# First stage of layer 0: the modulation of k tile 15 taken from TensorE to VectorE, in pieces of 256 columns

## The chip, the cores and the metric

The kernel runs on one core of one Trainium2 chip. The metric is the device time of one execution in microseconds (us). TensorE multiplies matrices, VectorE and ScalarE work element by element, GpSimd does a few small operations, and SyncE issues the transfers (DMA) between the device's memory and the core's on-chip memory (SBUF); matmul results land in PSUM, in banks of 512 columns.

## What is computed

A trunk of two mixer layers over 256 latent and 256 context tokens of width 2048, in float32. The part that matters here is the start of a layer, for both token streams:

```python
shift, scale, gate = split(silu(c) @ w_mod[l] + b_mod[l], 3)      # silu(c_ctx) for the context stream
h = rmsnorm(x, g_pre[l]) * (1 + scale) + shift
proj = h @ w_in[l]                                                # 2048 x 5120 a layer
y = concatenate(gMLP(proj), window_attention(proj), fourier_mix(proj))
x = x + gate * rmsnorm(y @ w_out[l], g_post[l])
```

`w_mod` is 2048 x 6144 a layer, and `c` has just one row a stream, so that product reads many bytes for little arithmetic.

## The kernel before, in words

Tokens lie along the columns: `h` is kept as 16 k tiles of 128 rows (channels) by 512 columns (256 latent, then 256 context tokens). Every float32 operand of the large products is split into a high and a low part (`hh`/`hl` for `h`, `whi`/`wlo` for weights), and `mm3` multiplies three of the four combinations. ScalarE makes the high part (L401, L505), VectorE the low part (L403, L510).

**The first stage** of layer 0 is the loop over k in `layer(0)`: the pass for one k is called step k here. A step multiplies h tile k with its rows of the weights: 12 matmuls into the four banks `av` and 9 into the three banks `au`. The h tiles are not there beforehand; each is made one step earlier, and for this its scale and shift have to be known. `mod_start` does that for one k tile: it loads 2 MB of `w_mod` (array `wsl`: for each of 16 tiles four blocks of 128 partitions x 4 rows x 256 columns, 128 of the columns scale and 128 shift), multiplies it on TensorE (L169: 16 matmuls a tile, four of them side by side in quarters of 32 columns), turns the result on VectorE (L173), adds the four quarters up with four tiny matmuls against `selq` (L178), and finishes scale (`gs`, L187, L189) and shift (`sh`, L190) on VectorE. `make_h` then makes `w2k` = x * gs * r (L501), `hh` (L505) and `hl` (L510).

From step 5 on, step k runs in this order: the first 6 `av` matmuls; the split of a piece of `w_in` into `whi` and `wlo`; the 16 modulation matmuls of tile k+2 (L169); the four of L178 for tile k+1 and `make_h` of tile k+1; the turn (L173) of tile k+2; the other 6 `av` matmuls; the 9 `au` matmuls.

**What sets the order.** TensorE's order is written out by hand for the whole kernel. VectorE's, ScalarE's and SyncE's are too until step 14, where `first_stage.close()` hands them to the compiler's scheduler; the operations that it may place begin a little before that point. Each engine takes its instructions in order. SyncE issues every load of this stage in order, and each issue waits until its buffer is free and until the eighth load before it has landed. Even tiles load into `mraw`, `mraw`, `macc`, `vv` (512 KB each), odd ones into `mg`, `mgl` and four pieces of 256 KB (in `hh`/`hl`, later `yo`); so the loads of tile k+2 wait for the matmuls of tile k. Pieces of `w_in` (512 KB) go through `raw`, which has 3 buffers, and become `whi`/`wlo`, which have 4 each. `LOADS` and `SPLITS` list how many pieces are loaded and split in each step.

Later modulation (layer 0's gate, layer 1's shift and scale) is done by VectorE already, in `mod_dve`: a running sum over the 16 rows with the element of silu(c) as scalar (L205, L207), then a turn and a reduction (L213, L214).

Of the kernel before, what the change touches and what calls it, by code (L numbers as in the profile page):

```python
# [7 lines left out]
F32 = mybir.dt.float32  # L8
# [3 lines left out]
ALU = mybir.AluOpType  # L12

P = 128
D = 2048
KT = D // P
# [50 lines left out]
def trunk_kernel(ctx: ExitStack, tc: tile.TileContext, xT, xhalf, cT, wss, wsl, wmod, win, wout0, wout1, const, vec, rows,  # L67
                 wmat, bs, sink, out):
    nc = tc.nc
    V, A, G, PE, DMA = nc.vector, nc.scalar, nc.gpsimd, nc.tensor, nc.sync  # L70
# [6 lines left out]
    def sb(shape, dt, tag, bufs=1):  # L77
        cnt[0] += 1
        return pool.tile(shape, dt, tag=tag, bufs=bufs, name=f"{tag}_{cnt[0]}")

    def w2k(shape, dt=F32):
        return sb(shape, dt, "w2k", W2K)
# [5 lines left out]
    def ms_ps(name="ms"):  # L88
        cnt[0] += 1
        return psum.tile([P, 512], F32, tag="ms", bufs=2, name=f"ps_{name}_{cnt[0]}")  # L90
# [12 lines left out]
    cs = sb([P, KT, 2], F32, "cs")  # L103
# [16 lines left out]
    def cc(name):  # L120
        o, w = COFF[name]
        return cst[:, o - P:o - P + w]

    def vc(l, name):
        o, w = VOFF[name]
        return vecs[:, l, o:o + w]
# [5 lines left out]
    gs = [sb([P, KT, 2], F32, f"gs{l}") for l in range(2)]  # L132
    sh = [sb([P, KT, 2], F32, f"sh{l}") for l in range(2)]
# [56 lines left out]
        V.tensor_tensor(out=sh[0][:, sl], in0=v[:, nk:2 * nk], in1=wide(bm[:, sl]), op=ALU.add)  # L190

    banks = {}

    def mod_dve(l, cb, red):

        acc = sb([P, 2, 512], F32, "macc")
        for kg in range(4):
            for kk in range(4):
                if kk % 2 == 0:
                    w = sb([P, 2, 512], F32, "mraw", 2)  # L200
                    DMA.dma_start(w, wmod[(cb - 8) if l == 0 else 4 + cb, kg][:, kk:kk + 2])
                for s in range(2):
                    c = cs[:, kg * 4 + kk, s:s + 1]
                    if kg == 0 and kk == 0:
                        V.tensor_scalar(out=acc[:, s], in0=w[:, kk % 2], scalar1=c, scalar2=None, op0=ALU.mult)  # L205
                    else:
                        V.scalar_tensor_tensor(out=acc[:, s], in0=w[:, kk % 2], scalar=c, in1=acc[:, s],  # L207
                                               op0=ALU.mult, op1=ALU.add)
                if kk % 2 and (kg < 3 or kk < 3):
                    yield  # L210
        t = sb([P, 2, 512], F32, "mraw", 2)
        for s in range(2):
            V.transpose(t[:, s], acc[:, s])  # L213
            V.tensor_reduce(out=red[:, s], in_=t[:, s].rearrange("p (b j) -> p b j", j=32),  # L214
                            axis=mybir.AxisListType.X, op=ALU.add)
        yield
# [264 lines left out]
    def new_h(k):  # L481
        hh[k] = sb([P, T], F32R, f"hh{k}")
        hl[k] = sb([P, T], F32R, f"hl{k}")

    def h_of(l, k, sl):

        if l == 0:
            return hh[k][:, sl], hl[k][:, sl]
        s, a = sl.start // S, sl.start % S
        t, b = (hh, hl)[s][k], a + sl.stop - sl.start  # L490
        return t[:, a:b], t[:, S + a:S + b]

    def make_h(l, k, rb, streams, between=()):

        if streams[0] == 0:
            new_h(k)
        t = w2k([P, T])
        for s in streams:
            sl = slice(s * S, (s + 1) * S)
            rsl = slice((s - streams[0]) * S, (s - streams[0] + 1) * S)  # L500
            V.scalar_tensor_tensor(out=t[:, sl], in0=yo[k][:, sl], scalar=gs[l][:, k, s:s + 1],  # L501
                                   in1=rb[:, rsl], op0=ALU.mult, op1=ALU.mult)
        for s in streams:
            sl = slice(s * S, (s + 1) * S)
            first = A.activation(h_of(l, k, sl)[0], t[:, sl], AF.Identity, bias=sh[l][:, k, s:s + 1])  # L505
        next(iter(between), None)
        for s in streams:
            sl = slice(s * S, (s + 1) * S)
            hi, lo = h_of(l, k, sl)
            last = V.scalar_tensor_tensor(out=lo, in0=t[:, sl], scalar=sh[l][:, k, s:s + 1],  # L510
                                          in1=hi.bitcast(F32), op0=ALU.add, op1=ALU.subtract)
        return first, last
# [58 lines left out]
    def layer(l):  # L571
        last = l == 1
        n = S if last else T
# [3 lines left out]
        if last:  # L577
            a = sb([P, 4, 256], F32, "macc")
            c = [sb([P, 2, S], F32, f"kt{j}") for j in range(2)]
# [35 lines left out]
        if l == 0:  # L615
            made = {}

            def mod_in(k, n=5):
                if k < KT:
                    g = made.setdefault(k, mod_start(k, 1))  # L620
                    for _ in range(n):
                        next(g, None)

            for k in range(KT):
                def take_in(n):
                    mod_in(k + 1, n)

                def splits():
                    for _ in range(SPLITS[k]):
                        W.emit()  # L630

                def h_next():

                    if k + 1 < KT:
                        mod_in(k + 1)
                        make_h(0, k + 1, rb0, [0, 1])

                if k % 2 == 0:
                    take(k)
                if k <= EARLY:  # L640
                    take_in(1)
                if k >= EARLY:
                    mod_in(k + 2, 1)
                for _ in range(LOADS[k]):
                    W.load()
                if k == 0:
                    start_av(0, range(nt))
                    take_in(3)
                    e = W.emitting(512)
                    next(e)  # L650
                    next(e)
                    take_in(2)
                    take(0, (1,))
                    start_au(0, (0,))
                    h_next()
                    list(e)
                    start_au(0, (1,))
                    warm(au[2], 3)
                elif k < MIDDLE:
                    start_av(k, range(nt // 2))  # L660
                    take_in(2)
                    start_av(k, range(nt // 2, nt))
                    take_in(1)
                    splits()
                    take_in(2)
                    start_au(k, (0,))
                    h_next()
                    start_au(k, (1,))
                    if k == 1:
                        warm(au[2], 4)  # L670
                    else:
                        ws_[2] = W.next()
                        for i in range(k + 1):
                            start_au(i, (2,))
                else:
                    start_av(k, range(nt // 2))
                    if k <= EARLY:
                        take_in(3)
                        splits()
                        take_in(2)  # L680
                        start_av(k, range(nt // 2, nt))
                        h_next()
                    else:
                        if k == KT - 2:
                            first_stage.close()
                        if k + 2 < KT:
                            banks["mod", k + 2] = banks["modc", k + 1] = ms_ps("mod")
                        splits()
                        mod_in(k + 2, 4)
                        if k + 1 < KT:  # L690
                            mod_in(k + 1)
                            make_h(0, k + 1, rb0, [0, 1])
                        mod_in(k + 2, 1)
                        start_av(k, range(nt // 2, nt))
                    if k >= KT - 2:
                        for _ in range(2):
                            with low(LAG), tc.issue_after(W.last.ins):
                                next(mods)
                    take(k, (1, 2))
                    start_au(k)  # L700
                    if k == EARLY:
                        mod_in(k + 2, 5)
# [26 lines left out]
        ws = sb([P, 4, P], F32, "ws")  # L729
# [3 lines left out]
        bsb = sb([P, 4, P], F32, "bsb")  # L733
# [193 lines left out]
        for h in range(len(au), 4):  # L927
            ps = tunit1([0])[0] if last else tunit(n, ps=ms_ps("t"))
# [7 lines left out]
        for h in range(4):  # L936
            ps = tunit1([0])[0] if last else tunit(n)
            gate(h, ps)
        state["phase"] = f"cg{l}"
        for g in range(4):  # L940
            ps = tunit1([0])[0] if last else tunit(n)
# [3 lines left out]
        r = sb([P, 4, S], F32, "mgl")  # L945
# [9 lines left out]
        for k in range(KT):  # L955
            if k % 4 == 0:
                w = W.next()
            c = slice((k % 4) * 256, (k % 4 + 1) * 256)
# [9 lines left out]
        for h in range(8):  # L968
            ps = tunit1([0])[0] if last else tunit(n)
# [3 lines left out]
        for h in range(8):  # L973
            ps = tunit1([0])[0] if last else tunit(n)
# [221 lines left out]
    with tc.manual_schedule(engines={EN.PE}):  # L1196
# [12 lines left out]
        for k in range(KT):  # L1209
            q = w2k([P, T])  # L1210
# [3 lines left out]
            c = slice(32 * (k % 4), 32 * (k % 4) + 32)  # L1214
# [10 lines left out]
        ps = ms_ps("rs")  # L1225
# [99 lines left out]
```

## Time and profile before

| | |
|---|---|
| median of 3 runs | 1141.86 us (1141.32 to 1142.33) |
| profiled execution, its own time | 1142.52 us |
| its span, first to last instruction | 1140.8 us |
| granted TensorE clock | 0.998 of full speed |
| TensorE matmul busy | 1126.3 us, 99% of the span |
| VectorE busy | 880.3 us, 77% |
| ScalarE busy | 515.9 us, 45% |
| DMA, mean over the span | 205 GB/s |
| first stage | from about 21 us to 139 us of the span |

The profile names engines PE (TensorE matmul), PEld (its weight load), DVE (VectorE), ACT (ScalarE), POOL (GpSimd) and SP (SyncE; SPq is its queue of DMA issues). A row of the timeline gives the start in the span, the duration, the engine, the line of the kernel, the operation, the tile written and the tiles read, the count, and in brackets the idle time before it and what ended that. A row of the DMA issues gives the count, the size of one and the median time from issue to landing. A row of the windows gives for a stretch of time each engine's busy time (with the number of instructions), the granted clock, the mean busy share of the 16 DMA engines and the bytes moved a second.

### The profile page before, as it was taken

What the parts mean: (1) busy time and instruction counts of PE and PEld (TensorE: products, weight loads), DVE (VectorE), ACT (ScalarE), POOL (GpSimd) and SP (SyncE); (2) the same over time, 40 slices, a digit from 0 to 9 for tenths busy, and PEclk for the clock granted to TensorE, in tenths of its full rate; (3) what the DMA queues carried; (4) which work ended last, traced back from release to release, by engine and by line L of the source; (5) the groups of instructions that cost most, each with busy time, mean ns of one, the idle gap of its engine ahead of it and who ended that gap; (6) DMA issues with size and microseconds to landing.
All of it is one profiled execution on the core that took longest, in us unless ns stands there. A gap on an engine that the chain in (4) does not pass through costs nothing.

```text
span 1140.8 us, 16858 instructions
## 1 busy us (share of the span) xinstructions
PE 1126.3 (99%) x6339; PEld 931.5 (82%) x6339; DVE 880.3 (77%) x1480; ACT 515.9 (45%) x933; POOL 31.6 (3%) x39
## 2 busy tenths in 40 slices
PE   8999999999999999999999999999999999999997
PEld 3567788888898888888888888888888988888885
DVE  1545499999987797889999893395789789868884
ACT  5222422322335666632532323366465369856550
POOL 0000000000000000000000000200500000000001
PEclk9999999999999999999999999999999999999999
DMA  9999666556655343355466654255865786556972
GB/s 351 395 387 404 240 202 198 182 186 218 195 182 169 112 138 130 108 197 189 147 219 217 206 185 149 74 188 185 198 223 180 239 275 194 167 160 199 300 255 74
DMA packets 72658, 234.28 MB, mean 205 GB/s; under 512 B 8448, under 2 KB 11392, under 8 KB 72576
## 3 DMA queue, kind: packets, MB, share of 16 engines
q1 hardware_dynamic: 70272, 231.11, 60.2%
q0 software_dynamic: 2304, 2.10, 1.3%
q8 instruction: 49, 0.80, 0.3%
q14 instruction: 33, 0.27, 0.1%
HBM read 231.08 MB, written 2.10 MB: 204 GB/s over the span
## 4 chain that ended last, share of the span: by engine, by line
PE 92%; DMA 4%; DVE 3%; ACT 1%; issue 1%; POOL 0%; SPq 0%; DVEq 0%; ACTq 0%; POOLq 0%
PE ps_t L423 14%; PE ps_t L425 14%; PE ps_t L424 14%; PE ps_t L539 8%; PE ps_t L540 4%; PE ps_y L423 3%; PE ps_y L425 3%; PE ps_y L424 3%; PE ps_mod L169 2%; PE ps_av L423 2%; PE ps_av L424 2%; PE ps_av L425 2%; PE ps_tp L906 2%; PE ps_cx L423 1%; PE ps_cx L425 1%; PE ps_cx L424 1%
## 5 line engine op out<-in xcount | busy, mean ns | idle before, releaser
L401 ACT CAST whi<-raw 128x1024 fp32r<-128x1024 f32 (+1 forms) x216 | 224.1, 1041 | 327.6 <-PE ps_t L424 186.4
L403 DVE TENSOR_TENSOR wlo<-raw,whi 128x1024 fp32r<-128x1024 f32 (+1 forms) x216 | 260.6, 1211 | 69.4 <-ACT whi L401 67.7
L423 PE MATMUL ps_t<-hh,whi 128*128 128x512 f32 (+1 forms) x704 | 268.2, 381 | 0.0
L425 PE MATMUL ps_t<-hh,wlo 128*128 128x512 f32 (+1 forms) x704 | 267.6, 380 | 0.0
L424 PE MATMUL ps_t<-hl,whi 128*128 128x512 f32 (+1 forms) x704 | 267.4, 380 | 0.0
L207 DVE SCALAR_TENSOR_TENSOR macc<-mraw,cs,macc 128x512 f32<-128x512 f32 x360 | 249.2, 747 | 16.3 <-DMA mraw<-in_wmod_dram 15.9
L539 PE MATMUL ps_t<-hh,whi 128*128 128x512 f32 x448 | 163.4, 402 | 0.0
L425 PEld LDWEIGHTS ps_t<-hh,wlo 128*128 128x128 f32 x704 | 132.4, 188 | 25.2
L423 PEld LDWEIGHTS ps_t<-hh,whi 128*128 128x128 f32 x704 | 132.4, 188 | 24.9 <-issue 1.2
L424 PEld LDWEIGHTS ps_t<-hl,whi 128*128 128x128 f32 x704 | 132.4, 188 | 23.8
L540 PE MATMUL ps_t<-hh,wlo 128*128 128x256 f32 x448 | 125.6, 280 | 0.3 <-DVE wlo L403 0.3
L539 PEld LDWEIGHTS ps_t<-hh,whi 128*128 128x128 f32 x448 | 84.2, 188 | 18.9 <-issue 0.5
L540 PEld LDWEIGHTS ps_t<-hh,wlo 128*128 128x128 f32 x448 | 84.6, 189 | 1.5 <-DVE wlo L403 1.0
L505 ACT ACTIVATE hh<-w2k,sh 128x256 fp32r<-128x256 f32 x48 | 21.8, 502 | 78.0 <-DVE w2k L501 78.0
L423 PE MATMUL ps_y<-whi,hh 128*128 128x512 f32 x104 | 41.3, 397 | 0.0
L425 PE MATMUL ps_y<-whi,hh 128*128 128x512 f32 x104 | 40.6, 390 | 0.0
L424 PE MATMUL ps_y<-wlo,hh 128*128 128x512 f32 x104 | 40.5, 389 | 0.0
L423 PE MATMUL ps_av<-whi,hh 128*128 128x512 f32 x96 | 39.7, 413 | 0.6 <-ACT hh L505 0.6
L423 PE MATMUL ps_cx<-whi,hh 128*128 128x512 f32 x96 | 38.9, 405 | 0.0
L424 PE MATMUL ps_av<-wlo,hh 128*128 128x512 f32 x96 | 38.0, 396 | 0.4 <-DVE wlo L403 0.4
L424 PE MATMUL ps_cx<-wlo,hh 128*128 128x512 f32 x96 | 37.4, 389 | 0.0
L440 ACT CAST w2k<-ps_tp 128x512 fp32r<-128x512 f32 x40 | 23.4, 585 | 23.2 <-PE ps_scc L424 12.7
(398 smaller groups left out, 1861.1 us busy)
## 6 DMA issues: line engine op xcount, KB each, us to landing
raw<-in_win_dram SPq DMA_DIRECT2D x160, 512.0 KB, 4.2
mraw<-in_wmod_dram SPq DMA_DIRECT2D x128, 512.0 KB, 4.4
raw<-in_wout_dram SPq DMA_DIRECT2D x60, 512.0 KB, 4.4
mraw<-in_wsl_dram SPq DMA_DIRECT2D x16, 512.0 KB, 7.4
yo<-in_xT_dram SPq DMA_DIRECT2D x16, 256.0 KB, 5.4
macc<-in_wsl_dram SPq DMA_DIRECT2D x8, 512.0 KB, 7.8
vv<-in_wsl_dram SPq DMA_DIRECT2D x8, 512.0 KB, 8.1
mg<-in_wsl_dram SPq DMA_DIRECT2D x8, 512.0 KB, 8.1
```

Source lines behind the costliest of these rows:

```text
L169: PE.matmul(ps[32 * kk:32 * kk + 32, 0:n], cpad[:, kg * 4 + kk], ws[kk], start=kg == 0, stop=kg == 3, tile_position=(0, 32 * kk))
L207: V.scalar_tensor_tensor(out=acc[:, s], in0=w[:, kk % 2], scalar=c, in1=acc[:, s], op0=ALU.mult, op1=ALU.add)
L401: A.copy(ph, rc)
L403: self.last = V.tensor_tensor(out=pl, in0=rc, in1=ph.bitcast(F32), op=ALU.subtract)
L423: PE.matmul(ps, st[0], mv[0], start=start, stop=False)
L424: PE.matmul(ps, st[0], mv[1], start=False, stop=False)
L425: PE.matmul(ps, st[1], mv[0], start=False, stop=stop)
L440: A.copy(hi, src)
L505: first = A.activation(h_of(l, k, sl)[0], t[:, sl], AF.Identity, bias=sh[l][:, k, s:s + 1])
L539: PE.matmul(ps, w[0], h, start=k == 0, stop=False)
L540: PE.matmul(ps[:, 0:S], w[1], h[:, 0:S], start=False, stop=k == KT - 1)
L906: PE.transpose(tp[:, (2 * j + b) * P:(2 * j + b + 1) * P], src, ident)
```

## The change

Tile 15 no longer goes through `mod_start`. Its 2 MB come as eight loads of 256 KB (`wide_load`, two rows of 256 columns for each partition), one in each of steps 3 to 10, behind the load of the `w_in` piece and ahead of the next tile's modulation loads. VectorE adds each of them in the step after (`wide_step`, steps 4 to 11): four operations on 128 x 256 a step, 32 in all. Behind `make_h` of step 12 it turns and reduces the two sums (`wide_turn`), and in step 14 four tiny matmuls and three small operations finish scale and shift (`wide_end`).

```diff
+    WIDE = {k: 1 for k in range(4, 12)}
+    def wide_load(n):
...
+            w = sb([P, 2, 256], F32, ("nstrh", "nstrl", "ws", "bsb")[i % 4])
+            DMA.dma_start(w, wsl[KT - 1, i // 2][:, 2 * (i % 2):2 * (i % 2) + 2])
...
+    def wide_step(n):
...
+            for k in (2 * i, 2 * i + 1):
+                for s in range(2):
+                    acc, c = wide["acc"][:, s], cs[:, k, s:s + 1]
+                    if k == 0:
+                        V.tensor_scalar(out=acc, in0=w[:, 0], scalar1=c, scalar2=None, op0=ALU.mult)
+                    else:
+                        V.scalar_tensor_tensor(out=acc, in0=w[:, k % 2], scalar=c, in1=acc, op0=ALU.mult, op1=ALU.add)
+    def wide_turn():
...
+        for s in range(2):
+            V.transpose(t[:, s], wide["acc"][:, s])
+            V.tensor_reduce(out=wide["red"][:, 0, s, 0:8], in_=t[:, s].rearrange("p (b j) -> p b j", j=32),
+                            axis=mybir.AxisListType.X, op=ALU.add)
+    def wide_end():
...
+        for q in range(4):
+            PE.matmul(ps[32 * q:32 * q + 32, 0:4], cc("selq"), r[:, :, :, q], start=True, stop=True,
+                      tile_position=(0, 32 * q))
...
             def mod_in(k, n=5):
-                if k < KT:
+                if k < KT - 1:
...
                 for _ in range(LOADS[k]):
                     W.load()
+                wide_load(WIDE.get(k + 1, 0))
+                more = WIDE.get(k, 0)
...
-                        if k + 2 < KT:
+                        if k + 2 < KT - 1:
                             banks["mod", k + 2] = banks["modc", k + 1] = ms_ps("mod")
+                        wide_step((more + 1) // 2)
                         splits()
+                        wide_step(more // 2)
                         mod_in(k + 2, 4)
                         if k + 1 < KT:
                             mod_in(k + 1)
+                            if k == KT - 2:
+                                wide_end()
                             make_h(0, k + 1, rb0, [0, 1])
+                        if k == max(WIDE) + 1:
+                            wide_turn()
```

The helpers stand 52 lines further down than before, the loop some 54 to 61. The order of the instructions moves at three places that the prediction speaks of.

TensorE in step 13, before: between the two halves of the `av` matmuls stand the 16 modulation matmuls of tile 15 (rows of L169) and the four tiny ones for tile 14 (L178).

```order
L425 MATMUL ps_av_280<-whi_1146,hl_257_1244 128x512
L169 MATMUL ps_mod_1289<-mg_1269,kt_24_87 32x256 x4
L169 MATMUL ps_mod_1289<-mgl_1271,kt_24_87 32x256 x4
L169 MATMUL ps_mod_1289<-yo_262_1273,kt_24_87 32x256 x2
L169 MATMUL ps_mod_1289<-yo_263_1275,kt_24_87 32x256 x2
L169 MATMUL ps_mod_1289<-yo_264_1277,kt_24_87 32x256 x2
L169 MATMUL ps_mod_1289<-yo_265_1279,kt_24_87 32x256 x2
L178 MATMUL ps_mod_1289<-w2k_1252,cst_79 32x4 x4
L423 MATMUL ps_av_281<-whi_1146,hh_256_1243 128x512
```

The same place now:

```order
L476 MATMUL ps_av_280<-wlo_1196,hh_265_1292 128x512
L477 MATMUL ps_av_280<-whi_1195,hl_266_1293 128x512
L178 MATMUL ps_modc_1336<-w2k_1307,cst_79 32x4 x4
L475 MATMUL ps_av_281<-whi_1195,hh_265_1292 128x512
L476 MATMUL ps_av_281<-wlo_1196,hh_265_1292 128x512
```

The 16 matmuls are gone; TensorE's order is otherwise what it was.

SyncE's queue in steps 5 and 6, before: a piece of `w_in`, the four loads of tile 8, another piece, the first loads of tile 9.

```order
L381 DMA raw_707<-in_win_dram 128x1024
L162 DMA mraw_769<-in_wsl_dram 128x1024
L162 DMA mraw_771<-in_wsl_dram 128x1024
L162 DMA macc_773<-in_wsl_dram 128x1024
L162 DMA vv_775<-in_wsl_dram 128x1024
L381 DMA raw_777<-in_win_dram 128x1024
L162 DMA mg_839<-in_wsl_dram 128x1024
```

The same place now, with two of the eight loads for tile 15 (L202, into `ws` and `bsb`):

```order
L433 DMA raw_716<-in_win_dram 128x1024
L202 DMA ws_718<-in_wsl_dram 128x512
L162 DMA mraw_784<-in_wsl_dram 128x1024
L162 DMA mraw_786<-in_wsl_dram 128x1024
L162 DMA macc_788<-in_wsl_dram 128x1024
L162 DMA vv_790<-in_wsl_dram 128x1024
L433 DMA raw_792<-in_win_dram 128x1024
L202 DMA bsb_794<-in_wsl_dram 128x512
L162 DMA mg_860<-in_wsl_dram 128x1024
```

Each tile's loads now stand behind one more load of 256 KB; tile 15's own six loads behind tile 14's are gone.

ScalarE and VectorE at the end of the stage. ScalarE before: the high part of tile 13, tile 14 with one weight piece between them (`whi`), two weight pieces, tile 15.

```order
L505 ACTIVATE hh_256_1243<-w2k_1245,sh_28_92 128x256 x2
L401 CAST whi_1290<-raw_1211 128x1024
L505 ACTIVATE hh_270_1317<-w2k_1319,sh_28_92 128x256 x2
L401 CAST whi_1352<-raw_1281 128x1024
L401 CAST whi_1408<-raw_1343 128x1024
L505 ACTIVATE hh_278_1364<-w2k_1366,sh_28_92 128x256 x2
```

ScalarE now (`m0r` is the attention mask):

```order
L557 ACTIVATE hh_265_1292<-w2k_1294,sh_28_92 128x256 x2
L453 CAST whi_1332<-raw_1260 128x1024
L453 CAST whi_1377<-raw_1324 128x1024
L453 CAST whi_1433<-raw_1368 128x1024
L557 ACTIVATE hh_275_1344<-w2k_1346,sh_28_92 128x256 x2
L557 ACTIVATE hh_282_1389<-w2k_1391,sh_28_92 128x256 x2
L786 CAST m0r_1475<-w2k_1473 128x128
```

VectorE there before, from the turn of tile 14 to the low part `hl` of tile 14:

```order
L173 STREAM_TRANSPOSE w2k_1252<-ps_mod_1219 128x256
L403 TENSOR_TENSOR wlo_1291<-raw_1211,whi_1290 128x1024
L187 SCALAR_TENSOR_TENSOR gs_26_90<-ps_mod_1289,vecs_78 128x2
L189 TENSOR_TENSOR gs_26_90<-gs_26_90,vecs_78 128x2
L190 TENSOR_TENSOR sh_28_92<-ps_mod_1289,vecs_78 128x2
L501 SCALAR_TENSOR_TENSOR w2k_1319<-yo_15_75,gs_26_90,acc_241 128x256 x2
L510 SCALAR_TENSOR_TENSOR hl_271_1318<-w2k_1319,sh_28_92,hh_270_1317 128x256 x2
```

VectorE now:

```order
L173 STREAM_TRANSPOSE w2k_1307<-ps_mod_1268 128x256
L455 TENSOR_TENSOR wlo_1333<-raw_1260,whi_1332 128x1024
L187 SCALAR_TENSOR_TENSOR gs_26_90<-ps_modc_1336,vecs_78 128x2
L455 TENSOR_TENSOR wlo_1378<-raw_1324,whi_1377 128x1024
L189 TENSOR_TENSOR gs_26_90<-gs_26_90,vecs_78 128x2
L190 TENSOR_TENSOR sh_28_92<-ps_modc_1336,vecs_78 128x2
L553 SCALAR_TENSOR_TENSOR w2k_1346<-yo_15_75,gs_26_90,acc_241 128x256 x2
L455 TENSOR_TENSOR wlo_1434<-raw_1368,whi_1433 128x1024
L562 SCALAR_TENSOR_TENSOR hl_276_1345<-w2k_1346,sh_28_92,hh_275_1344 128x256 x2
```

Two more weight splits now stand in front of tile 14's `hh` on ScalarE and in front of its `hl` on VectorE; they stood behind them before.

More of the change, by code (lines that the diff above doesn't have):

```diff
@@ L192, in trunk_kernel, with both @@
     banks = {}
+    wide = {"n": 0, "w": []}
+    WIDE = {k: 1 for k in range(4, 12)}
+    def wide_load(n):
+        for _ in range(n):
+            i = wide["n"]
+            wide["n"] += 1
+            w = sb([P, 2, 256], F32, ("nstrh", "nstrl", "ws", "bsb")[i % 4])
+            DMA.dma_start(w, wsl[KT - 1, i // 2][:, 2 * (i % 2):2 * (i % 2) + 2])
+            wide["w"].append((i, w))
+    def wide_step(n):
+        if "acc" not in wide:
+            wide["acc"] = sb([P, 2, 256], F32, "ctrh")
+        for _ in range(n):
+            i, w = wide["w"].pop(0)
+            for k in (2 * i, 2 * i + 1):
[6 more added lines that the diff above has]
+    def wide_turn():
+        wide["red"] = sb([P, 4, 2, 16], F32, "red", 2)
+        t = sb([P, 2, 256], F32, "nstrh")
+        for s in range(2):
[3 more added lines that the diff above has]
+    def wide_end():
+        ps = ms_ps("modc")
+        r = wide["red"][:, 0, :, 0:8].rearrange("p s (j q) -> p s j q", q=4)
+        for q in range(4):
+            PE.matmul(ps[32 * q:32 * q + 32, 0:4], cc("selq"), r[:, :, :, q], start=True, stop=True,
+                      tile_position=(0, 32 * q))
+        v = ps[:, 0:4].rearrange("p (s j) -> p j s", s=2)
+        k, bm = KT - 1, vc(0, "bmod")
+        def both(c):
+            return c.to_broadcast([P, 2])
+        V.scalar_tensor_tensor(out=gs[0][:, k], in0=v[:, 0], scalar=1.0, in1=both(bm[:, KT + k:KT + k + 1]),
+                               op0=ALU.add, op1=ALU.add)
+        V.tensor_tensor(out=gs[0][:, k], in0=gs[0][:, k], in1=both(vc(0, "gpre")[:, k:k + 1]), op=ALU.mult)
+        V.tensor_tensor(out=sh[0][:, k], in0=v[:, 1], in1=both(bm[:, k:k + 1]), op=ALU.add)
     def mod_dve(l, cb, red):
@@ L678, in layer @@
                         take_in(3)
+                        wide_step(more)
                         splits()
```

## The prediction

> **What bounds the kernel now.** I read the page's busy table first, then TensorE's waits over the whole span, then the windows and TensorE's timeline of the first stage, then the issues and landings of its loads. Page, then TensorE's waits (total us, times, longest):
>
> ```profile
> span 1140.8 us, 16858 instructions
> PE 1126.3 (99%) x6339; PEld 931.5 (82%) x6339; DVE 880.3 (77%) x1480; ACT 515.9 (45%) x933; POOL 31.6 (3%) x39
> ...
> PE ps_t L539 <- DVE hl L510: 1.0, 1, 1.0
> PE ps_rs L1215 <- ACT w2k L1211: 0.9, 1, 0.9
> PE ps_rs L461 <- DVE acc L1167: 0.7, 1, 0.7
> ```
>
> TensorE has work for 99% of the span and no wait longer than about 1 us after the opening: what the first stage gains or loses on TensorE passes to the end nearly one to one. So everything hangs on TensorE between 50 and 139 us. The windows of that stretch (DMA share and GB/s stand last):
>
> ```profile
> 52.00:54.00 2.00, 2.00 (x33) 1.08 (x26) 0.99 (x2) 0.00 (x0) 0.00 (x0) 1.00 1.06 327
> 54.00:56.00 2.00, 2.00 (x16) 1.39 (x15) 0.66 (x5) 0.00 (x0) 0.00 (x0) 1.00 0.89 341
> ...
> 60.00:62.00 2.00, 2.00 (x25) 1.24 (x18) 0.45 (x1) 0.00 (x0) 0.00 (x0) 1.00 0.73 246
> ...
> 64.00:66.00 2.00, 2.00 (x25) 1.21 (x27) 1.00 (x3) 1.60 (x3) 0.00 (x0) 1.00 0.97 328
> ...
> 70.00:90.00 20.00, 20.00 (x179) 14.78 (x175) 11.09 (x28) 5.65 (x10) 0.00 (x0) 1.00 1.03 407
> 90.00:110.00 20.00, 20.00 (x175) 14.75 (x171) 10.85 (x27) 5.56 (x9) 0.00 (x0) 1.00 1.04 403
> ```
>
> TensorE never stops, but the DMA engines are full as well from 70 us on, at 403 to 407 GB/s. The stage has two bounds a hair apart.
>
> **What goes: 16 matmuls.** TensorE's timeline, start of the second `av` half of steps 12, 13 and 14:
>
> ```profile
> 118.69 0.50 PE L423 MATMUL ps_av<-whi,hh 128*128 128x512 f32 x1
> ...
> 125.61 0.50 PE L423 MATMUL ps_av<-whi,hh 128*128 128x512 f32 x1
> ...
> 130.81 0.50 PE L423 MATMUL ps_av<-whi,hh 128*128 128x512 f32 x1
> ```
>
> From 118.69 to 125.61 (6.92 us) stand 21 main matmuls, 16 modulation matmuls (tile 15) and four tiny ones; from 125.61 to 130.81 (5.20 us) the same without the 16. The change turns the first kind into the second: **−1.72 us**, the whole of what can be won. Step 14 keeps its four tiny matmuls, now fed by `wide_end`.
>
> **What is added to the load queue.** The 2 MB are the same, but they come earlier: eight loads of 256 KB ahead of tiles 5 and 7 to 13, in a stretch where the DMA engines have nothing left. At 405 GB/s one takes 0.26 MB / 0.405 = 0.65 us, and whatever stands behind it lands that much later. The idle shares above give some of it back: against 1.03, they lack 0.28 us (54 to 56), 0.60 (60 to 62) and 0.12 (64 to 66), together 1.0 us; counted by bytes against 405 GB/s, with 52 to 54, they lack 1.9 us. That is room for two or three of the first three loads, and none after it. Whether TensorE feels the rest is read from the last load of a tile, against the matmuls that need it. Tile 10: issue, time to landing, use; then tile 11 and tile 13, whose last matmul group starts 0.22 us before the tiny matmuls (16 matmuls take 1.05 us in four groups):
>
> ```profile
> 80.36 0.33 SPq L162 DMA_DIRECT2D vv<-in_wsl_dram  x1
> vv<-in_wsl_dram SPq DMA_DIRECT2D x1, 512.0 KB, 9.0
> 90.40 0.40 PE L169 MATMUL ps_mod<-vv,kt 128*32 128x256 f32 x4
> ...
> 88.09 0.33 SPq L162 DMA_DIRECT2D yo<-in_wsl_dram  x1
> yo<-in_wsl_dram SPq DMA_DIRECT2D x1, 256.0 KB, 7.8
> 97.75 0.22 PE L178 MATMUL ps_mod<-w2k,cst 128*32 128x4 f32 x8
> ...
> 101.06 0.33 SPq L162 DMA_DIRECT2D yo<-in_wsl_dram  x1
> yo<-in_wsl_dram SPq DMA_DIRECT2D x1, 256.0 KB, 7.8
> 110.74 1.05 PE L169 MATMUL ps_mod<-yo,kt 128*32 128x256 f32 x16
> 111.61 0.22 PE L178 MATMUL ps_mod<-w2k,cst 128*32 128x4 f32 x8
> ```
>
> Tile 10's last load lands at 89.4 and is used at 90.40: 1.0 us to spare. Tile 11's lands at 95.9, used at 97.53: 1.6. Tile 13's lands at 108.9, used at 111.39: 2.5. Ahead of them stand five, six and eight of the new loads: 3.25, 3.9 and 5.2 us, less 1.0 to 1.9. So tile 10 comes 0.35 to 1.25 us late, tile 11 no later than that, and tile 13 0.8 to 1.7 us (the lateness is one delay that grows, not a sum, since a TensorE that waited once has moved back for all later tiles). I take **+1.2 us**, the middle for tile 13. Ends for the range: 0 if the queue finds more room than its idle shares show, 2.7 (5.2 − 2.5) if it finds none.
>
> By the Trainium skill, "DMA: Bandwidth & Descriptors", Specifications, about 358 GB/s is the limit of a core on the memory side; by that figure a load would take 0.73 us and tile 13 would come up to 3.4 us late. The rows at 403 to 407 GB/s disagree, and the page's own single-core measurement of large transfers lies above 400 too.
>
> **What is added to VectorE.** The nearest rows for the new operations, and VectorE around step 11, where two weight splits leave the least room:
>
> ```profile
> L501 DVE SCALAR_TENSOR_TENSOR w2k<-yo,gs,acc 128x256 f32<-128x256 f32 x28 | 12.3, 482 | 0.0
> L214 DVE TENSOR_REDUCE red<-mraw 128x16 f32<-128x512 f32 x24 | 15.7, 670 | 0.1
> ...
> 107.28 0.44 DVE L173 STREAM_TRANSPOSE w2k<-ps_mod 128x256 f32<-128x256 f32 x1
> 107.82 2.36 DVE L403 TENSOR_TENSOR wlo<-raw,whi 128x1024 fp32r<-128x1024 f32 x2
> 111.98 0.16 DVE L187 SCALAR_TENSOR_TENSOR gs<-ps_mod,vecs 128x2 f32<-128x2 f32 x1 [1.80 <-PE ps_mod L178]
> ```
>
> Two operations of 128 x 256 on three operands are 12.3 / 14 = 0.88 us, so the four of a step take 1.76 to 1.93 us. In step 11 VectorE waits 1.80 us for TensorE's tiny matmuls; the four fit there, or are 0.13 us over. In the other steps one split stands instead of two, so 1.2 us more is free. Cost: **0**, hidden by that wait, and where TensorE itself is late by the queue the wait is longer still; without the cover the worst is 0.13 us, and never a gain. The pieces themselves land in time: each stands right behind the weight piece and is first needed a step later. The turn in step 12 is two of 0.44 us and two reductions of at most 0.67 (half the columns), 1.6 to 2.2 us, in a step whose VectorE otherwise only turns tile 14 and splits one piece: 0, at worst 0.2 if the turn of tile 14 comes behind TensorE.
>
> **What is moved at the end of the stage.** ScalarE's third `whi` of those rows may only be written when step 13 has used the buffer's old piece, and tile 14's `hh` and `hl` now stand behind it. Durations and TensorE's clock there:
>
> ```profile
> L401 ACT CAST whi<-raw 128x1024 fp32r<-128x1024 f32 x11 | 11.2, 1037 | 0.0
> L403 DVE TENSOR_TENSOR wlo<-raw,whi 128x1024 fp32r<-128x1024 f32 x11 | 13.2, 1220 | 1.0 <-ACT whi L401 0.5
> L510 DVE SCALAR_TENSOR_TENSOR hl<-w2k,sh,hh 128x256 fp32r<-128x256 f32 x28 | 12.4, 484 | 2.5 <-ACT hh L505 2.4
> ...
> 120.31 0.88 DVE L510 SCALAR_TENSOR_TENSOR hl<-w2k,sh,hh 128x256 fp32r<-128x256 f32 x2 [0.18 <-ACT hh L505]
> ...
> 127.11 0.39 PE L423 MATMUL ps_au<-hh,whi 128*128 128x512 f32 x1
> 129.16 0.39 PE L423 MATMUL ps_av<-whi,hh 128*128 128x512 f32 x1
> ```
>
> Call E the end of step 13's second `av` half (127.11 before, 125.39 without the 16 matmuls). Step 14 starts at E + 2.05 (129.16 − 127.11) and needs `hl` of tile 14 in its third matmul, at E + 2.5. VectorE: tile 13's `hl` is done at 121.19, E − 4.2; the turn and reductions bring it to E − 2.5, the turn of tile 14 to E − 2.1, the first split to E − 0.9, `gs`, the second split and `sh` to E + 0.7, `w2k` to E + 1.6. The third `whi` is ready at E + 1.04, so it does not delay the third split, which ends at E + 2.8; the first half of `hl` follows at E + 3.3. TensorE waits **+0.8 us** there. `hh`, at E + 1.8, is in time. Ends: 0.3, if the operations overlap by 0.1 us each, as back-to-back rows do (0.88 for two of 0.48); 1.4, if reductions and waits on its own results take the upper values. Before, `hl` stood in front of both splits.
>
> Later stages: TensorE's order is unchanged there; VectorE's sums for the gate move by some places around 140 to 190 us, with TensorE waiting for none of them: 0, plus or minus 0.5.
>
> **Sum.** −1.72 + 1.2 + 0 + 0.8 = +0.3 us on the profiled execution, whose 1142.52 us are its span of 1140.8 and 1.7 around it, 0.66 above the median. On the median: 1141.86 + 0.3 = **1142.2 us**.
>
> **The rivals.** Within 0.2% (2.3 us, about what a measurement of this kernel can tell from no change) means 1139.6 to 1144.1.
>
> *The gain arrives whole.* The queue takes up all eight loads and tile 14's `hl` is in time: −1.72 to −1, about 1140.4 us. For it: the landings hold 1.0 to 2.5 us of spare time. Against it: five to eight loads of 0.65 us are more than that. Even then it is 0.15%, no faster than 0.2%.
>
> *The loads cost by count, not by bytes (slower).* If a load of 256 KB holds the queue nearly as long as one of 512 KB (1.3 us at 405 GB/s), eight take 10.4 us; less 1.9 of idle and 2.5 spare, tile 13 comes 6.0 us late, and with 0.8 of tile 14: −1.72 + 6.0 + 0.8 = +5, 1147 us. It decides from 0.9 us a load: 8 x 0.9 − 1.9 − 2.5 = 2.8, and 2.8 + 0.8 − 1.72 is 1.9, with the upper end for tile 14 already 2.5. Against it: tiles of six loads and tiles of four took turns at 403 and 407 GB/s. The Trainium skill's rule ("DMA: Bandwidth & Descriptors", Rules for kernel authors: at least 1 MiB a DMA for the highest bandwidth) speaks for this rival; the windows above, full at that rate with loads of 256 and 512 KB, show no such loss.
>
> *No spare room in the queue.* 2.7 + 0.8 to 1.4 − 1.72 = +1.8 to +2.4: 1143.7 to 1144.3 us, on the edge of 0.2%.
>
> *Later order.* VectorE's other order beyond 140 us moves a wait elsewhere: plus or minus 3 us.
>
> **Chances.** Forecast (−1 to +1.7) 0.60; gain whole 0.16; no room 0.12, half of it over the edge; by count 0.05; later order 0.07, split 0.03 faster, 0.04 slower. Two hundredths of the whole gain may add up with later order to pass the edge. Faster 0.05, slower 0.06 + 0.05 + 0.04 = 0.15, same 0.80. The range runs from the gain kept nearly whole, 1140.3, to the upper end without room, 1144.3.
>
> **What would show it.** In the profile of the changed kernel: L169's matmuls 16 fewer; step 13 5.2 us long; DMA still full at 403 to 407 GB/s from 60 to about 110 us and empty earlier than before; TensorE's weight loads for tile 10 and tile 13 (L169) waiting for a DMA, about 1.2 us in all; the third `av` matmul of step 14 waiting about 0.8 us for `hl`; VectorE's wait ahead of L187 short in steps 5 to 11 but not gone. I am wrong if L169 waits for nothing or for over 2.7 us, if `gs` is late in step 11, or if TensorE's gaps past 140 us change by more than 0.5 us.

## The result and the profile after

The changed kernel takes 1145.74 us (median of 20 runs, 1143.85 to 1150.72), the kernel before 1142.38 us beside it (1141.01 to 1145.03): a ratio of 1.0032, 95% interval 1.0024 to 1.0040. It is slower by 3.4 us, and above the range given.

The profiled execution of the changed kernel took 1143.90 us, the second fastest of its twenty; that of before, 1142.52, lies close to its median. The two profiles differ by 1.4 us, the medians by 3.4: this profile shows less than half of the loss. First what it does show. Its span and busy row:

```profile
span 1142.1 us, 16816 instructions
PE 1126.7 (99%) x6303; PEld 931.0 (82%) x6307; DVE 892.1 (78%) x1515; ACT 516.0 (45%) x933; POOL 31.7 (3%) x39
```

The windows of the first stage (last columns: granted clock, DMA share, GB/s) and the waits from 60 to 132 us (us in total, times, longest), VectorE's wait ahead of `gs` before in a block of its own behind them:

```profile
70.00:90.00 20.00, 20.00 (x163) 14.55 (x157) 15.10 (x40) 5.64 (x10) 0.00 (x0) 1.00 1.03 403
90.00:110.00 20.00, 20.00 (x180) 14.37 (x179) 13.20 (x38) 5.25 (x9) 0.00 (x0) 1.00 1.03 402
...
120.00:130.00 10.00, 10.00 (x70) 7.53 (x58) 8.66 (x21) 4.65 (x7) 0.00 (x0) 1.00 0.52 181
```

```profile
DVE gs L187 <- PE ps_mod L178: 15.4, 8, 4.2
...
PEld ps_mod L169 <- DMA vv<-in_wsl_dram: 0.8, 2, 0.4
...
PEld ps_mod L169 <- DMA yo<-in_wsl_dram: 0.6, 3, 0.3
...
PE ps_av L477 <- DVE hl L562: 0.3, 1, 0.3
```

```profile
DVE gs L187 <- PE ps_mod L178: 26.7, 9, 4.2
```

The queue is full at the same rate, and now TensorE's weight loads of L169 wait for it. VectorE's wait ahead of `gs`, 26.7 us before, still stands at 15.4: the added operations fit. TensorE at the end of the stage (start, duration, idle time before it):

```profile
125.85 0.50 PE L475 MATMUL ps_av<-whi,hh 128*128 128x512 f32 x1
...
129.63 0.40 PE L476 MATMUL ps_av<-wlo,hh 128*128 128x512 f32 x1
130.34 0.50 PE L477 MATMUL ps_av<-whi,hl 128*128 128x512 f32 x1 [0.32 <-DVE hl L562]
```

The third `av` matmul of step 14 waits for tile 14's `hl`. Up to here all is as in the prediction's steps. What was not in them stands 600 us later, in layer 1. ScalarE and TensorE there, before:

```profile
749.61 0.51 ACT L505 ACTIVATE hh<-w2k,sh 128x256 fp32r<-128x256 f32 x1 [1.77 <-DVE w2k L501]
...
750.19 1.05 ACT L401 CAST whi<-raw 128x1024 fp32r<-128x1024 f32 x1
```

and in the changed kernel:

```profile
750.10 0.51 ACT L557 ACTIVATE hh<-w2k,sh 128x256 fp32r<-128x256 f32 x1 [1.76 <-DVE w2k L553]
...
751.46 1.05 ACT L453 CAST whi<-raw 128x1024 fp32r<-128x1024 f32 x1 [0.84 <-DMA raw<-in_win_dram]
...
754.22 0.50 PE L477 MATMUL ps_av<-whi,hh 128*128 128x512 f32 x1 [0.33 <-DVE hh L562]
```

A weight piece arrives late, ScalarE's cast waits 0.84 us for it, and TensorE falls back at 753 us. The change has no instruction anywhere near.

### The profile page after: what moved, and what is told of

Same layout as the page of the kernel before. It is cut to its first block, busy times and chain, and to the rows that moved or that the text cites. A ratio compares the mean times of both kernels' runs of the same rounds, so it can differ in the third digit from the quotient of the medians.

```text
span 1142.1 us, 16816 instructions
## 1 busy us (share of the span) xinstructions
PE 1126.7 (99%) x6303; PEld 931.0 (82%) x6307; DVE 892.1 (78%) x1515; ACT 516.0 (45%) x933; POOL 31.7 (3%) x39
## 4 chain that ended last, share of the span: by engine, by line
PE 89%; DMA 4%; DVE 4%; ACT 2%; issue 1%; SPq 0%; POOL 0%; DVEq 0%; ACTq 0%; POOLq 0%
PE ps_t L475 14%; PE ps_t L477 14%; PE ps_t L476 14%; PE ps_t L591 8%; PE ps_t L592 4%; PE ps_y L475 3%; PE ps_y L477 3%; PE ps_y L476 3%; PE ps_mod L169 2%; PE ps_av L475 2%; DMA raw<-in_win_dram 2%; PE ps_av L477 2%; PE ps_av L476 2%; PE ps_tp L967 1%; PE ps_cx L475 1%; PE ps_cx L477 1%
```

## The experiments

Every run has its median against the kernel before on the same chip, and one profile. To read the profiles, each matmul of a kernel is set beside the same matmul in before's profile; its lateness is its start less the start before, and the table gives by how much TensorE's lateness grows in four stretches (before's times): 51 to 114 us (loads of the first stage), 114 to 150 (the removed matmuls, and tile 14's `hl`), 150 to 760, and 760 to the last common matmul. The last columns are explained with e6. Times in us.

| kernel | ratio to before, 95% | 51–114 | 114–150 | 150–760 | 760–1132 | instruction load at | first `raw` load near 747 took | growth at 753 |
|---|---|---|---|---|---|---|---|---|
| before | 1 | 0 | 0 | 0 | 0 | 742.2 | 3.6 | 0 |
| after | 1.0032 (1.0024–1.0040) | 1.75 | −1.12 | 0.28 | −0.07 | 748.3 | 4.3 | 0.49 |
| e1 | 1.0035 (1.0021–1.0049) | 1.36 | −1.14 | 1.55 | 1.55 | 748.4 | 4.5 | 0.65 |
| e2 | 1.0006 (0.9997–1.0014) | 0.00 | −1.14 | 1.68 | 1.94 | 748.6 | 5.1 | 1.13 |
| e4 | 1.0024 (1.0009–1.0038) | 2.13 | −1.70 | 0.75 | 1.05 | 748.5 | 4.3 | 0.48 |
| e5 | 1.0018 (1.0010–1.0027) | 1.41 | 0.00 | 0.38 | 1.10 | 742.9 | 3.6 | 0 |
| e6 | 1.0007 (0.9997–1.0018) | 2.23 | −1.12 | −0.28 | −1.02 | 742.7 | 3.4 | 0 |
| e7 | 1.0033 (1.0022–1.0045) | 0.23 | 0.00 | 0.99 | 3.28 | 752.3 | 4.8 | 0.89 |
| e7b | 1.0020 (1.0011–1.0028) | 0.00 | 0.00 | −0.13 | 0.13 | 749.9 | 3.5 | 0 |
| e8 | 0.9986 (0.9977–0.9994) | 0.88 | −0.77 | −0.25 | −0.17 | 742.5 | 3.6 | 0 |
| e8 again | 1.0001 (0.9992–1.0009) | 0.86 | −0.77 | −0.28 | −1.07 | 742.0 | 3.7 | 0 |
| e9 | 0.9996 (0.9987–1.0005) | 0.00 | −0.77 | −0.25 | −1.17 | 740.0 | 3.5 | 0 |
| e10 | 0.9991 (0.9982–1.0000) | 1.01 | −1.12 | −0.28 | −0.31 | 741.9 | 3.7 | 0 |
| e11 | 0.9998 (0.9990–1.0007) | 0.00 | −0.78 | −0.27 | 0.52 | 742.2 | 3.6 | 0 |
| e12 | 0.9998 (0.9990–1.0007) | 0.00 | 0.00 | −0.13 | −1.20 | 738.7 | 3.5 | 0 |

The first theory (Q) was that the whole loss is the load queue's, the rival (O) that it is the changed order of VectorE and ScalarE.

**e1**, the changed kernel again.

> The changed kernel itself, unaltered, as a control on the chip of the runs beside it and for a second profile. Theory Q (the eight added loads leave the load queue no spare time, so that what loading varies by from execution to execution becomes waiting of TensorE): about +3.4 us over the kernel before, executions spread over about 7 us where the kernel before has 4; a profile of an execution that takes over 1145 us shows the extra time before 120 us, as waits of L169 or L477 for a DMA. Theory O (the order at the end of the stage or later costs more than the first profile shows): the same time, but the extra time stands after 120 us.

The time repeats (1146.73). Its profile is of an execution of 1145.83 us, and the extra time stands after 150 us, against Q: 3.1 us. One part of it is VectorE's order, as O has it. VectorE and TensorE at 158 to 169 us:

```profile
158.00 0.75 DVE L259 SCALAR_TENSOR_TENSOR macc<-mraw,cs,macc 128x512 f32<-128x512 f32 x1 [1.77 <-DMA mraw<-in_wmod_dram]
...
164.25 4.05 DVE L259 SCALAR_TENSOR_TENSOR macc<-mraw,cs,macc 128x512 f32<-128x512 f32 x6
...
168.22 0.74 DVE L820 SCALAR_TENSOR_TENSOR w2k<-ps_mix,vecs,bsb 128x512 f32<-128x512 f32 x1
...
169.02 1.16 PE L818 MATMUL ps_mix<-ws,w2k 128*128 128x128 f32 x8 [0.74 <-DVE w2k L820]
```

Six sums for the gate now stand in one row ahead of the `w2k` that TensorE needs (before, five did, and that `w2k` waited 0.45 us for TensorE, not the other way round); when a load of `mraw` comes late, TensorE falls back 0.9 us at 168. The order alone does not do it: in the first profile the same kernel has the same six sums, and TensorE does not wait there.

**e2**, one piece instead of eight; **e4**, the hand order closed one step later; **e5**, the kernel before with the eight loads alone.

```
e2  -  w = sb([P, 2, 256], F32, (...)[i % 4]); DMA.dma_start(w, wsl[KT - 1, i // 2][...])
    +  if i == 0:
    +      w = sb([P, 2, 256], F32, "ws"); DMA.dma_start(w, ...); wide["one"] = w
    +  w = wide["one"]
e4  -  if k == KT - 2:
    +  if k == KT - 1:
           first_stage.close()
e5  +  if 3 <= k < 11:                      # behind W.load() of step k
    +      w = sb([P, 2, 256], F32, (...)[(k - 3) % 4]); DMA.dma_start(w, wsl[KT - 1, ...])
```

> The changed kernel with one load of 256 KB instead of eight; all 32 operations of VectorE read that one piece. Left out: seven of the eight loads, so tile 15's modulation is not that of the reference. Theory Q: the 16 matmuls' 1.72 us come back, less 0.5 for tile 14's hl: -1.2 us against the kernel before (1141.2), with its spread of about 4 us. Theory O, or VectorE's added operations as the cause: no change against the changed kernel, about +3.4 us over before.

> The changed kernel with the hand order of the first stage held one step longer (closed at step 14's end of order, not at step 13's), so that tile 14's hh and hl stand ahead of the third pair of weight splits. Theory Q: at most the 0.5 us that the first profile shows as waiting for hl come back, so about +2.9 us over before, spread as wide as the changed kernel's. Theory O: most of the +3.4 us goes, to within 1 us of before.

> The kernel before with the eight loads of 256 KB alone, in steps 3 to 10 where the change has them; nothing reads them, TensorE, VectorE and ScalarE work as before. Theory Q: the 16 matmuls are still there and no hl is late, so the changed kernel's +3.4 plus 1.72 less 0.5: about +4.6 us over before, spread as wide as the changed kernel's. Theory O: no change against before, within 0.5 us.

In the first stage all three do what Q says: without the seven loads nothing waits for a DMA (e2, 0.00) and 1.14 us are gained there; without the late `hl` it is 1.70 (e4); the loads alone cost 1.41 (e5). e4's time, 0.24% over before, is Q's too. But e2's median is 2.1 us above Q's figure (1143.34 for 1141.2), and e5's 0.18% over before, 2.1 us, is less than half of Q's 4.6: the loads do not make up the loss. In e2 and e4, as in e1, TensorE loses 1.8 to 3.6 us behind 150 us, part of it at one place in all: 753 us, where e5 loses nothing. What the four profiles that lose there (after, e1, e2, e4) share, and e5 has not, is a TensorE program with 32 matmuls and 32 weight loads less.

**e6**. TensorE's instructions come by DMA too: the page lists 49 loads of 16 KB of a kind "instruction" in one queue, in both kernels (packets, MB, share of the engines):

```profile
q8 instruction: 49, 0.80, 0.3%
```

That these are TensorE's follows from their number and, below, from how they move with its program. 12,678 weight loads and matmuls over 49 are 259 instructions a load, one every 22.5 us; 64 instructions fewer put every later one a quarter of that, 5.6 us, later in the program. At 742 us, where the 33rd of them stands in the kernel before, hardly anything else moves (3 GB/s from 740 to 745 us); in the changed kernel it stands at 748.3, where data is loaded. Theory C is that at its new place it delays the data load that it meets. e6 gives the program its length back by cutting idle matmuls of the start; e7 moves the loads in the kernel before, by three quarters of a load the other way.

```
 def warm(ps, n):
     for _ in range(n):
-        PE.matmul(ps, wz[:, 0:P], wz, start=True, stop=True)
+        m = 2 if idles[0] > 0 else 1       # e6: the first 32; e7: 4 for 2
+        idles[0] -= 1
+        for i in range(m):
+            c = slice(i * T // m, (i + 1) * T // m)
+            PE.matmul(ps[:, c], wz[:, 0:P], wz[:, c], start=True, stop=True)
```

> The changed kernel with 32 of the idle matmuls of the first 24 us (128x512, their result unused) cut into two halves of 256 columns each: the same columns, 32 more matmuls and weight loads, as many as the change took away, so that TensorE's later instruction loads (16 KB by a DMA of about 1 us, every 23 us or so) come at the same places of the program as in the kernel before. Theory C (a part of the loss comes from these loads, which the change shifts by 6 to 9 us onto other data transfers, as at 748 us): the 0.5 to 1.1 us of waiting at 753 us goes, and most of what stands at 956 and 1114 us; about +2.4 us over the kernel before instead of +3.6. Theory Q and O: no change against the changed kernel.

> The kernel before with 32 of the idle matmuls of the first 24 us cut into four quarters of 128 columns each: 96 more matmuls and weight loads, three quarters of an instruction load, so that the later loads fall where they fall in the changed kernel. Nothing else differs. Theory C: a wait of 0.5 to 1.1 us at 753 us, something at 956 and 1114 us, in all +1 to +1.5 us over the kernel before. Theory Q and O: the kernel before's time, within 0.4 us.

e6 takes 1143.53 us, 0.07% over before (one of its eleven executions, of 1547.41 us, is not in the ratio): of the 0.32% three quarters are gone, more than C gave, and its interval (to 1.0018) ends below those of the changed kernel (from 1.0024 and, in e1, from 1.0021). Its first stage is no better than the changed kernel's (2.23 and −1.12); the gain lies behind 150 us. The DMA view of the changed kernel, 747.0 to 747.5 us (an issue: KB, us to landing) and 748 to 750:

```profile
raw<-in_win_dram SPq DMA_DIRECT2D x1, 512.0 KB, 4.3
```

```profile
q1 hardware_dynamic: 135, 0.52, 76.0%
q8 instruction: 1, 0.02, 4.1%
```

and of e6, 742 to 744 us, 747.5 to 748 us, and ScalarE's cast:

```profile
q8 instruction: 1, 0.02, 3.0%
```

```profile
raw<-in_win_dram SPq DMA_DIRECT2D x1, 512.0 KB, 3.4
```

```profile
751.07 1.05 ACT L453 CAST whi<-raw 128x1024 fp32r<-128x1024 f32 x1
```

The table's last columns show the same in all fifteen profiles: where the instruction load starts well inside the first `raw` load, that takes 4.3 to 5.1 us and TensorE loses 0.5 to 1.1 at 753 (five profiles); elsewhere it takes 3.4 to 3.7 and nothing is lost (ten, e7b among them, where it starts half a microsecond before the landing). At 168 us e6 does not wait, with the same VectorE order as e1; but neither does the first profile of the changed kernel, so that place tells less. Ahead of it `mraw` took 5.4 to 6.1 us in the four profiles with an instruction load inside it (after, e1, e2, e4) and 5.0 in e6 and e10.

A second place bears theory C out. The last load of `w_out`, issued between 1105 and 1116 us, took 4.6 to 5.3 us in the six profiles in which an instruction load starts inside it (after, e1, e2, e4, e7, e7b), and 3.4 to 3.6 us in the nine others. In e4 it took 5.0 and ScalarE and TensorE wait for it; before it took 3.4:

```profile
raw<-in_wout_dram SPq DMA_DIRECT2D x1, 512.0 KB, 5.0
```

```profile
1115.66 1.14 ACT L453 CAST hl<-raw 128x512 fp32r<-128x512 f32 x2 [3.31 <-DMA raw<-in_wout_dram]
1116.34 0.50 PE L475 MATMUL ps_y<-hl,hh 128*128 128x512 f32 x1 [0.74 <-ACT hl L453]
```

```profile
raw<-in_wout_dram SPq DMA_DIRECT2D x1, 512.0 KB, 3.4
```

TensorE falls back 1.5 us there in e4, 0.2 to 0.4 in e1, e2 and e7, and not at all in after and e7b, whose load was issued 1.8 and 2.9 us sooner than e4's and landed in time. At 956 us it falls back 0.5 us in after and 0.4 in e1. Neither loss is in e6, as its expectation had it.

e7 moved the loads and is slower by 3.8 us, but its profile, which is of the slowest of its twelve executions (1149.96 us), shows another reason for some of that: the granted clock (third from last in the windows) falls behind an idle gap, and TensorE is 2.9 us late by 45 us. It falls a second time, from 848.7 to 852.1 us, behind gaps of 0.39 and 0.74 us, and TensorE falls back 1.4 us more there. TensorE, and the windows:

```profile
17.80 0.64 PE L169 MATMUL ps_mod<-mraw,kt 128*32 128x256 f32 x8 [1.49 <-DMA mraw<-in_wsl_dram]
```

```profile
20.00:26.00 6.00, 6.00 (x44) 3.68 (x44) 0.56 (x2) 1.10 (x2) 1.03 (x1) 0.50 1.03 399
...
848.70:852.10 3.40, 3.40 (x15) 3.11 (x14) 2.88 (x8) 2.09 (x5) 1.06 (x1) 0.50 0.51 164
```

At 753 us it loses 0.89 us, as theory C had it.

**e7b**, e7 with the gap filled (six whole idle matmuls behind the sums of squares, and four of the cuts in halves).

> As e7 (the kernel before with TensorE's later instruction loads moved to about the changed kernel's places by cut idle matmuls), with six whole idle matmuls added behind the sums of squares, where e7's TensorE stood idle for 1.5 us and its granted clock then fell to 0.50 for 20 to 26 us. Theory C: the start costs nothing now, and the waits at 753 and 956 us of e7 stay: about +1 to +2 us over the kernel before. If e7's loss was the clock alone: no change against before, within 0.4 us.

The clock stays at 1.00 there:

```profile
20.00:26.00 6.00, 5.33 (x60) 3.12 (x60) 2.29 (x8) 1.88 (x4) 1.03 (x1) 1.00 1.03 398
```

The kernel is still slower than before, by 0.1 to 0.3%. Its profile, the second quickest of its executions, shows 0.4 us, all from the start, so this pair confirms the direction and no place.

**e10**, e2 with e6's cut, and **e12**, the kernel before with e6's cut.

> e2 (one piece loaded, read by all 32 operations; seven loads left out, so tile 15's modulation is not that of the reference) with the instruction loads brought back as in e6. Theory C, with the queue's part shown by e6: -1.73 + 0.48 = -1.2 us against the kernel before, about 1141.5, and no waits at 753 and 1114 us. Otherwise it stays at e2's +0.7.

> The kernel before with the same cut as e6 (32 idle matmuls in two halves each), as its control. If the cut itself is what makes e6 2.8 us faster than the changed kernel, this kernel is as much faster than before: about 1139.5 us. By theory C the cut gives nothing of its own; it moves the instruction loads a quarter of a load (5 to 7 us) ahead of their places in the kernel before, which can cost 0 to 2.5 us: +0 to +2.5 us, and not faster than before by more than 0.5.

e10 comes to 1141.57 us, as C has it. Its interval touches that of e2 (0.9997), and 0.15%, by which the two differ, is also what two runs of one kernel differ by below (e8), so this pair alone would not do; beside e6 it points the same way. e12 equals the kernel before: the cut gives nothing of its own, and instruction loads moved the other way (to 738.7 us) cost nothing here, so what a shift costs hangs on where the loads come to stand.

**e8, e9, e11**: half of tile 15 on VectorE, half on TensorE.

```
 # mod_start, tile 15
+first = 2 if k0 == KT - 1 else 0          # TensorE: groups 2 and 3 alone
-for kg in range(4):
+for kg in range(first, 4):
...
+if first:                                  # and VectorE's half into the same sum
+    PE.matmul(ps[...], cc("selq"), r8[:, :, :, q], start=False, stop=True, ...)
-WIDE = {k: 1 for k in range(4, 12)}
+WIDE = {k: 1 for k in range(4, 8)}         # e11: (4, 6, 8, 10)
```

> VectorE modulates half of tile 15 (contraction rows of the first four pieces, loaded in steps 3 to 6), TensorE the other half and adds both; the hand order closes at step 14's end, as in e4. Theory Q: four pieces are 2.6 us of loading against 3.1 to 3.8 of room (eight pieces' 5.2 less the 1.4 to 2.1 by which the four kernels with eight loads were late), so no step waits for a DMA; 8 calls, 0.86 us of TensorE, saved; nothing for hl. At 150 us the kernel stands 0.8 us ahead of before, measured from the first matmul of step 0. Theory C and O take 0.5 to 2 us of it later (168, 753, 1114 us): +0 to +1 us over before in all. If the pieces cost in proportion and not above a room, the first stage loses 0.7 to 1.0 us by waiting for loads and gains nothing.

> e8 (half of tile 15 on VectorE) with 8 idle matmuls cut in halves, so that TensorE has as many instructions as in the kernel before; in e8 it has 8 matmuls and 8 weight loads fewer, which puts the instruction loads 1 to 2 us later. If e8's -1.3 us is of its own (matmuls saved, no wait for hl): it stays, about 1141.5. If it comes from where the instruction loads fall: it goes, about 1142.8.

> e8 with its four loads in steps 3, 5, 7 and 9 instead of 3 to 6. e8's profile has 0.87 us of waiting at tiles 8 and 9, right behind the four loads. Theory Q (room per step): at most 0.3 us of that stays, so about 0.5 us less than e8, 1141.0. If the room is one for the whole stage, it stays as in e8.

> e8 again. If its lead is the kernel's: 0.998 to 0.999 of the kernel before, about 1141.3 us. If it was the draw of those runs: within 0.05% of before, as e9 and e11.

The first e8 was 0.14% faster than before; its repeat and the two siblings are not to be told from before. No version here beats it. The loads, though, behave as in e11's expectation: four at a stretch (steps 3 to 6) cost 0.87 us in both profiles, four spread out cost nothing. That e9, with four at a stretch, also lost nothing, and e10, with one, lost 1.0 us at tile 7, shows that the queue's spare room differs between executions by about 1 us; so it is not shown that the spreading is what helped in e11.

## Why the prediction was wrong, step by step

- *Removed matmuls, −1.72.* Measured −1.73, in every profile that has the change. (They are 16 calls and 32 records of L169, where the forecast said 16.) Step 13 is 5.20 us long, as said.
- *Loads, +1.2 (0 to 2.7).* Mis-sized, inside its ends: 1.36 to 2.23 in the four profiles with eight loads and the change, 1.8 by the ratios (e6 less e10, seven loads, 0.16%). The wait does stand at L169, first at tile 10 in e1 and e5, as forecast, but at tile 7 or 8 in after, e4 and e6: the spare time read in one execution was not there in others. "By count", which put tile 13 at 6.0 us late, is refuted: eight loads cost no more than 2.2 us in any profile.
- *VectorE, 0.* Right: in e2, with all 32 operations, nothing before 125 us is late.
- *Tile 14's `hl`, +0.8 (0.3 to 1.4).* 0.48 at that matmul and 0.11 behind it; e4 takes it away.
- *Later stages, 0 ± 0.5.* **The step that failed.** It rested on TensorE's order being unchanged there, and did not ask where its instructions come from: 64 fewer of them move the instruction loads by 5.6 us onto data loads that had none. The part is 2.9 us by the ratios (1.0032 less 1.0007; their intervals leave about 1.5 us either way), more than the other two losses together; e2 less e10 gives 1.7 and e7b less before 2.3. Of this the profiles place 0.5 to 1.1 us at 753 us and up to 1.5 at 1114; where the rest stands is not shown. The rival "later order" was right in size, and VectorE's order has a part at 168 us in e1, e2 and e4 (0.35 to 0.9 us), though only with a late `mraw`.
- *The sum.* −1.73 + 1.8 + 0.6 = +0.7 us at the end of the stage, forecast +0.3; then 2.9: 3.6, measured 3.4.

What stays open: how one load of 16 KB (about 1 us) makes one of 512 KB 0.6 to 1.7 us longer, since the trace does not tell the DMA engines apart; the stretch from 760 us on, where profiles of kernels with before's code places differ by 2 us among themselves, so that, but for the places named above, its share is known by the ratios alone; and the late `mraw` ahead of 168 us, which e8 and e11 have too (6.0 and 6.4 us, 5.4 to 6.1 in after, e1, e2 and e4) with no instruction load in it.

## What to carry to other kernels

An edit that takes instructions away moves the instruction loads of all that follows; where an effect as small as the 0.3% here is studied, give the program its old length back (here by cutting idle matmuls) and see what is left of it. And set a profile beside the times of all runs before reading it: the profile of a quick execution can hide just what the median pays.

## What the runs showed of the hardware

- Instruction loads of TensorE are data traffic: 16 KB each, 0.9 to 1.3 us in the kernel before, about 259 instructions, 49 in this program (50 with 192 instructions more, e7). At the two places compared in all fifteen profiles, a load of 512 KB with one of them well inside it took 4.3 to 5.3 us, the others 3.4 to 3.7. Where they fall is worth 2.9 us here by the ratios, give or take 1.5, about as much as the terms of the change itself.
- Behind an idle gap of TensorE of 1.49 us, ended at 17.8 us, the granted clock was 0.81 from 18 to 20 us and 0.50 from 20 to 26 us (e7); with that gap filled it stayed at 1.00 (e7b). A short gap does not always do this: the clock stayed at 1.00 behind 1.04 us at 879.7 us in the kernel before and 1.24 us at 882.1 in e1. The Trainium skill ("TensorE: Matmul & The Clock Gate", What's actually happening) has the clock fall after about 3.4 us without work; in e7 a shorter gap was enough, in a stretch of small matmuls.
